# Weight-block sums three units ahead of their splits in a Strassen-type feed-forward, and another order of its first units

## The chip, the core and the metric

The kernel runs on one core of a Trainium2 chip. Its time is device microseconds (us) of one launch; the median of several runs is given, and of one of its executions the hardware profiler took the trace that is read here. Engines are named as in the profile: PE is TensorE's matmul, PEld its weight load, DVE is VectorE, ACT is ScalarE, POOL is GpSimd, SP is SyncE, whose queue asks for the weight transfers.

## What is computed

Two layers of a decoder trunk on 256 tokens of width 1024, all in fp32. Each layer is a feed-forward (FFN), a mixer, a cross-attention and a second FFN:

```python
def swiglu(x, w_gate, w_up, w_down):
    return (jax.nn.silu(x @ w_gate) * (x @ w_up)) @ w_down

for l in range(DEPTH):
    h = h + 0.5 * swiglu(rms_norm(h, ffn1_norm[l]), ffn1_w_gate[l], ffn1_w_up[l], ffn1_w_down[l])
    h = h + hybrid_mixer(rms_norm(h, mix_norm[l]), w_in[l], ssm_lambda_re[l], ssm_lambda_im[l],
...
    h = h + memory_cross_attention(rms_norm(h, xattn_norm[l]), rms_norm(mem, mem_norm[l]),
...
    h = h + 0.5 * swiglu(rms_norm(h, ffn2_norm[l]), ffn2_w_gate[l], ffn2_w_up[l], ffn2_w_down[l])
return rms_norm(h, final_norm)
```

DEPTH is 2, D_MODEL 1024 and D_FF is 2816. Only the second FFN of each layer is touched.

## The kernel before

**Units.** Every weight matrix comes as a stream of blocks of 128 x 1024 fp32 (512 KB). One block makes one unit of work: SP asks for its transfer into a `raw` buffer (4 of them), ScalarE rounds it to a high part `whi`, VectorE subtracts that from the block and so makes a low part `wlo` (5 buffers of each), and TensorE multiplies with high and low parts of the activations, three matmuls (high x high, high x low, low x high) for each product wanted. A plain unit is 12 matmuls of 128 x 512. `split_whole` writes the two instructions that split a block, `load_to` asks for transfers up to a few units ahead.

**The order** of the work is written out by the program on the host: a planner (`Clock`) keeps a model of the time of each engine, and by it places splits, evacuations and matmuls one behind the other. Each engine then runs its own list in that order. `feed` writes the split of a unit when it is due, up to 4 us of the model ahead and as far as the 5 buffers go.

**The second FFN** has 11 chunks of 256 columns of gate and of up. Its order of units is the string `SECOND`: P4 is a unit of the gate-and-up projection of chunk 4 (four make a chunk), D0 one of the down projection of chunk 0 (two make a chunk, into PSUM tiles `acc`), S2 is one product of the pair of chunks 2 and 3. P's matmuls go to the PSUM tiles `mm` (2 buffers), which ScalarE and VectorE empty into `z` (silu times up); TensorE transposes z (`tp<-ident,z`), and ScalarE and VectorE split the result into `gT`, the operand of D.

**The pairs.** Chunks 2 and 3, and chunks 7 and 8, are each computed as one Strassen-type product: seven products of half matrices instead of eight. Each takes two units of 6 matmuls, and its result goes to a PSUM tile `tp`. The table `PAIR` holds them in order: Q3, Q1, Q7, Q6, Q2, Q5, Q4. The weight operands are four blocks, X, P, Y, Q, two units each, and sums of them that VectorE makes in place:

- Q3 uses X, Q1 uses P, Q2 uses Q as they are loaded.
- Q7 uses X after X = X + Y; Q6 uses X after X = X + P; Q5 uses Y after Y = Y + P; Q4 uses X after X = X + Q.

In the names of the profile these are `blkX`, `blkP`, `blkY`, `blkQ`; X and Y lie in fixed places, P and Q in a pool of twelve slots (`s4`). In `split_whole` the sum of a unit stands right ahead of its own split: sum on VectorE, high part on ScalarE, low part on VectorE. In `load_to` each of Q3, Q1, Q7 and Q2 brings one block (both its units); Q6, Q5 and Q4 bring none.

The activations' own combinations (`xf`, `ef`, then high and low parts `eh`, `el`) are made in `combos`, started when chunk 0 is projected; Q3 needs the first of them. The results of the seven products are copied or added into `qs` on ScalarE and VectorE, and `chunk_done` transposes them (`tp<-ident,qs`) into `gT`.

Lines: L268 is VectorE's recorder, L305 ScalarE's, L344 the matmul, L355 the transpose, L557 the weight transfers.

Of the kernel before, what the change touches and what calls it, by code (L numbers as in the profile page):

```python
# [11 lines left out]
F32 = mybir.dt.float32  # L12
# [4 lines left out]
ALU = mybir.AluOpType  # L17
# [31 lines left out]


SECOND = (
# [3 lines left out]
)  # L55

PAIR = (
    ("Q3", (1, 1), "X", "X", None),
    ("Q1", (0, 0), "P", "P", None),
    ("Q7", (1, 0), "Y", "X", "Y"),  # L60
    ("Q6", None, None, "X", "P"),
    ("Q2", (0, 1), "Q", "Q", None),
    ("Q5", None, None, "Y", "P"),
    ("Q4", None, None, "X", "Q"),
)


def second_items():

    seen = {}  # L70
    for item in SECOND.split():
        k = seen[item] = seen.get(item, -1) + 1
        yield item[0], int(item[1:]), k
# [29 lines left out]
def stream_plan():  # L103

    plan = []
    for l in range(L):
        def ffn(nm):
            for j in range(NCH):
                for kp in range(4):
                    plan.append((nm + "_gu", l, 4 * j + kp, "A", (nm, l, 2 * kp), 4 if j == 0 and len(plan) >= 4 else 1))  # L110
                if j >= LAG:
                    for f in range(2):
                        plan.append((nm + "_dn", l, 2 * (j - LAG) + f, "B", None, 1))
            for n in range(2 * (NCH - LAG), 2 * NCH):
                plan.append((nm + "_dn", l, n, "B", None, 2 * LAG))

        def second(nm):
            for kind, j, k in second_items():
                if kind == "P":
                    plan.append((nm + "_gu", l, 4 * j + k, "A", None, 4 if j == 0 else 1))  # L120
                elif kind == "D":
                    plan.append((nm + "_dn", l, 2 * j + k, "B", None, 1))
                else:
                    _, block, to, operand, add = PAIR[k]
                    for u in range(2):
                        n = None if block is None else 4 * (j + block[0]) + 2 * block[1] + u
                        plan.append((nm + "_gu", l, n, "S", ((l, j), u, to, operand, add), 1))
            for n in range(2 * (NCH - LAG), 2 * NCH):
                plan.append((nm + "_dn", l, n, "B", None, 2 * LAG))

        def chunk(nm, c, norm, skew):
            for kp in range(4):
                plan.append((nm, l, 4 * c + kp, "A", (norm, l, 2 * kp), skew))

        ffn("ffn1")
        for c in range(4):
            chunk("w_in", c, "mix", 4 if c == 0 else 1)
        for c in range(3):
            chunk("wkv", c, "mem", 1)
        for k in range(4):  # L140
            plan.append(("w_glu", l, k, "B", None, 4))
        for k in (4, 5, 6, 7, 0, 1, 2, 3):
            plan.append(("w_out", l, k, "B", ("ssm", l, k) if k < 4 else ("sub", l, 0), 4))
        for c in range(2):
            chunk("wq", c, "xattn", 4 if c == 0 else 1)
        chunk("wkv", 3, "mem", 1)
        for k in range(8):
            plan.append(("wo", l, k, "B", None, 4))
        second("ffn2")
    need, at, i = [], 0.0, 0  # L150
    while i < len(plan):
        n = plan[i][5]
        need += [at + STEP * k for k in range(n)]
        at += STEP if plan[i][3] == "S" else 2 * STEP * n
        i += n
    return plan, need


class Task:


    def __init__(self, gen, now):
        self.gen, self.t, self.done, self.waiters = gen, now, False, []
        self.pe = -1.0
# [195 lines left out]
class Trunk:  # L360
    def __init__(self, ctx, tc, io):
        self.tc, self.io = tc, io
        self.c = Clock(tc.nc)
        self.v, self.a, self.g, self.p = Vector(self.c), Scalar(self.c), Pool(self.c), Tensor(self.c)
        P = lambda name, bufs, **kw: ctx.enter_context(tc.tile_pool(name=name, bufs=bufs, **kw))
        self.const = P("const", 1)
        self.xp = P("xp", 2)
        self.rawp = P("raw", N_RAW)
        self.hip = P("hi", N_W)
        self.lop = P("lo", N_W)  # L370
        self.tab = P("tab", 1)
        self.s4 = P("s4", N_S4)
        self.zp = P("zp", 4)
        self.gp = P("gp", 2)
        self.tp5 = P("tp5", N_T5)
        self.jp = P("jp", 1)
        self.sm = P("sm", 4)
        self.sp1 = P("sp1", 1)
        self.acc = P("acc", 4, space=bass.MemoryType.PSUM)
        self.mm = P("mm", 2, space=bass.MemoryType.PSUM)  # L380
        self.tp = P("tp", 1, space=bass.MemoryType.PSUM)
        self.dram = P("dram", 1, space=bass.MemoryType.DRAM)
        self.plan, self.need = stream_plan()
        self.main = 0.0
        self.upos = self.nload = self.nsplit = self.nfree = 0
        self.raw, self.w, self.blk = {}, {}, {}
        self.stream = Task(None, 0.0)
        self.nacc = self.nmm = 0
        self.accfree = [0.0, 0.0]
        self.mmfree = [0.0, 0.0]  # L390
        self.tpfree, self.tpown = [0.0, 0.0], {}
# [131 lines left out]
    def split_whole(self, i):  # L523
        hi = self.hip.tile([128, 1024], F32R, tag="hi", name="whi")
        lo = self.lop.tile([128, 1024], F32R, tag="lo", name="wlo")
        self.stream.t = 0.0
        kind, op = self.plan[i][3:5]
        if kind == "S":
            pair, u, _, operand, add = op
            r = self.blk[pair, operand, u]  # L530
            if add is not None:
                self.v.tensor_tensor(r, r, self.blk[pair, add, u], op=ALU.add)
        else:
            r = self.raw.pop(i)
        self.split(hi, lo, r)
        self.w[i] = [hi, lo, self.stream.t, self.stream.t]

    def load_to(self, m):
        while self.nload < min(m, len(self.plan)):
            i = self.nload  # L540
            self.nload += 1
            _, _, n, kind, op, _ = self.plan[i]
            if n is None:
                continue
            if kind != "S":
                r = self.rawp.tile([128, 1024], F32, tag="raw", name="raw")
                self.raw[i] = r
            else:
                pair, u, to = op[:3]
                if to in "PQ":  # L550
                    r = self.s4t([128, 1024], name="blk" + to)
                else:
                    if u == 0:
                        self.blk[pair, to] = self.tab.tile([128, 2, 1024], F32, tag={"X": "tB", "Y": "tD"}[to], name="blk" + to)
                    r = self.blk[pair, to][:, u, :]
                self.blk[pair, to, u] = r
            self.tc.nc.sync.dma_start(r, self.io["wst"][self.nwst])  # L557
            self.nwst += 1

    def split_unit(self, i, q):  # L560
        kind, gain = self.plan[i][3:5]
# [1298 lines left out]
def lay_out(a):  # L1860
# [7 lines left out]
    def type_b(w):  # L1868
        return w.reshape(-1, 128, 1024)

    groups = {}
    for l in range(L):
        for nm in ("ffn1", "ffn2"):
            g = f[nm + "_w_gate"][l].reshape(D, NCH, 1, 256)
            u = f[nm + "_w_up"][l].reshape(D, NCH, 1, 256)
# [5 lines left out]
        groups["wo", l] = type_b(f["xattn_wo"][l])  # L1881
        groups["w_glu", l] = type_b(f["ssm_w_glu"][l])
        groups["w_out", l] = type_b(f["w_out"][l])
    wst = np.concatenate([groups[s, l][n:n + 1] for s, l, n, _, _, _ in stream_plan()[0] if n is not None], axis=0)
    col = lambda v: v.reshape(-1, 128).T
    gains = np.concatenate(
        [col(f[k][l]) for l in range(L)
# [30 lines left out]
```

## Time and profile before

| | |
|---|---|
| Median of 3 runs | 1239.87 us (1234.87 to 1244.61) |
| Profiled execution | 1238.06 us, span 1236.3 us |
| Second FFN of layer 0, first to last product | 444 to 588 us of the span |
| Second FFN of layer 1, first to last product | 1051 to 1197 us |
| Granted TensorE clock, mean of the span | 0.994 |

A row of a group gives the busy time and the mean of one instruction; a row of the waits gives who waited for whom, us in total, times, longest. A row of the timeline is start, duration, engine, line, operation, output<-inputs and, in brackets, how long its engine was idle before it and what ended that. TensorE's matmuls overlap: its pace is read from start to start.

### The profile page before, as it was taken

What the parts mean: (1) busy time and instruction counts of PE and PEld (TensorE: products, weight loads), DVE (VectorE), ACT (ScalarE), POOL (GpSimd) and SP (SyncE); (2) the same over time, 40 slices, a digit from 0 to 9 for tenths busy, and PEclk for the clock granted to TensorE, in tenths of its full rate; (3) what the DMA queues carried; (4) which work ended last, traced back from release to release, by engine and by line L of the source; (5) the groups of instructions that cost most, each with busy time, mean ns of one, the idle gap of its engine ahead of it and who ended that gap; (6) DMA issues with size and microseconds to landing.
All of it is one profiled execution on the core that took longest, in us unless ns stands there. A gap on an engine that the chain in (4) does not pass through costs nothing.

```text
span 1236.3 us, 17726 instructions
## 1 busy us (share of the span) xinstructions
PE 1201.5 (97%) x6580; PEld 973.4 (79%) x6580; DVE 904.8 (73%) x1498; ACT 711.1 (58%) x1206; POOL 45.1 (4%) x104
## 2 busy tenths in 40 slices
PE   9999999999999999998999999999999999999987
PEld 7888888777888877776888887887678888777766
DVE  5797776597867587867678877656977667786775
ACT  6665455567766555554555644655686656545543
POOL 2100001000000000000010000100000000000000
PEclk9999999999999999999999999999999999998999
DMA  8655557543644564453565655664445446545532
GB/s 282 214 187 182 163 151 208 150 140 117 194 159 145 184 224 153 172 186 119 184 200 183 193 160 160 186 192 141 125 160 175 155 149 225 174 151 213 166 114 86
DMA packets 59974, 210.91 MB, mean 171 GB/s; under 512 B 7168, under 2 KB 8288, under 8 KB 59888
## 3 DMA queue, kind: packets, MB, share of 16 engines
q1 hardware_dynamic: 56304, 202.92, 50.9%
q0 software_dynamic: 2000, 5.24, 1.4%
q10 hardware_dynamic: 1584, 1.62, 0.5%
q8 instruction: 51, 0.84, 0.3%
q14 instruction: 35, 0.29, 0.1%
HBM read 207.00 MB, written 1.05 MB: 168 GB/s over the span
## 4 chain that ended last, share of the span: by engine, by line
PE 81%; DVE 11%; ACT 4%; issue 2%; DMA 1%; ACTq 0%; POOLq 0%; POOL 0%; DVEq 0%
PE mm L344 42%; PE acc L344 29%; PE tp L344 6%; PE tp L355 5%; DVE wlo L268 5%; ACT whi L305 3%; DVE blkX L268 2%; DMA uq<-z 1%; DVE blkY L268 1%; DVE qs L268 1%; DVE p L268 1%; DVE gT L268 1%; DMA h<-in_x 0%; DVE z L268 0%; DVE xf L268 0%
## 5 line engine op out<-in xcount | busy, mean ns | idle before, releaser
L268 DVE SCALAR_TENSOR_TENSOR wlo<-raw,gains,whi 128x512 fp32r<-128x512 f32 x368 | 263.1, 747 | 92.9 <-ACT whi L305 91.5
L344 PE MATMUL mm<-whi,xh 128*128 128x512 f32 x768 | 308.0, 401 | 0.0
L344 PE MATMUL mm<-wlo,xh 128*128 128x512 f32 x768 | 300.6, 392 | 0.3 <-DVE wlo L268 0.3
L344 PE MATMUL mm<-whi,xl 128*128 128x512 f32 x768 | 300.8, 392 | 0.0
L305 ACT ACTIVATE whi<-raw,gains 128x512 fp32r<-128x512 f32 x368 | 240.9, 713 | 14.3 <-DMA raw<-in_wst 5.7
L344 PE MATMUL acc<-whi,gT 128*128 128x512 f32 (+1 forms) x712 | 237.7, 396 | 0.0
L268 DVE TENSOR_TENSOR wlo<-raw,whi 128x512 fp32r<-128x512 f32 (+1 forms) x236 | 209.0, 912 | 29.0 <-ACT whi L305 27.9
L305 ACT ACTIVATE whi<-raw 128x512 fp32r<-128x512 f32 (+1 forms) x236 | 181.0, 805 | 45.6 <-DMA raw<-in_wst 18.9
L344 PEld LDWEIGHTS mm<-whi,xh 128*128 128x128 f32 x768 | 145.3, 189 | 31.5 <-issue 1.3
L344 PEld LDWEIGHTS mm<-whi,xl 128*128 128x128 f32 x768 | 144.9, 189 | 30.8
L344 PEld LDWEIGHTS mm<-wlo,xh 128*128 128x128 f32 x768 | 145.3, 189 | 28.6 <-DVE wlo L268 0.8
L344 PEld LDWEIGHTS acc<-whi,gT 128*128 128x128 f32 x712 | 133.2, 188 | 26.6
L344 PE MATMUL acc<-wlo,gT 128*128 128x512 f32 (+1 forms) x356 | 138.0, 388 | 0.0
L344 PE MATMUL mm<-whi,mem 128*128 128x512 f32 x256 | 92.6, 409 | 0.0
L344 PEld LDWEIGHTS acc<-wlo,gT 128*128 128x128 f32 x356 | 67.1, 188 | 12.0
L305 ACT ACTIVATE sg<-mm,rstd 128x256 f32<-128x256 f32 x44 | 20.9, 474 | 87.1 <-PE mm L344 87.0
L305 ACT ACTIVATE whi<-blkX 128x1024 fp32r<-128x1024 f32 x32 | 33.6, 1057 | 55.0 <-DVE blkX L268 55.0
L268 DVE TENSOR_TENSOR wlo<-blkX,whi 128x1024 fp32r<-128x1024 f32 x32 | 39.2, 1225 | 33.7 <-ACT whi L305 33.7
L344 PEld LDWEIGHTS mm<-whi,mem 128*128 128x128 f32 x256 | 48.1, 188 | 11.5 <-issue 1.3
L344 PE MATMUL mm<-wlo,mem 128*128 128x512 f32 x128 | 50.9, 398 | 3.9 <-DVE wlo L268 3.9
L305 ACT ACTIVATE xh<-tp 128x512 fp32r<-128x512 f32 x32 | 19.1, 596 | 58.7 <-PE tp L355 58.7
L305 ACT ACTIVATE z<-mm,rstd 128x256 f32<-128x256 f32 (+1 forms) x52 | 29.4, 568 | 39.5 <-PE mm L344 38.9
(256 smaller groups left out, 1531.2 us busy)
## 6 DMA issues: line engine op xcount, KB each, us to landing
raw<-in_wst SPq DMA_DIRECT2D x350, 512.0 KB, 4.2
blkX<-in_wst SPq DMA_DIRECT2D x8, 512.0 KB, 5.2
blkP<-in_wst SPq DMA_DIRECT2D x8, 512.0 KB, 6.4
blkY<-in_wst SPq DMA_DIRECT2D x8, 512.0 KB, 5.6
blkQ<-in_wst SPq DMA_DIRECT2D x8, 512.0 KB, 5.4
raw<-in_wst SPq DMA_DIRECT2D x4, 256.0 KB, 5.4
mem<-in_mem POOLq DMA_DIRECT2D x2, 512.0 KB, 7.4
uq<-z ACTq DMA_DIRECT2D x8, 128.0 KB, 4.6
```

Of the source, the lines that this page charges most:

```text
L268: r = getattr(self.e, name)(*a, **k)
L305: r = self.e.activation(out, in_, func, **k)
L344: r = self.e.matmul(out, lhsT, rhs, **k)
L355: r = self.e.transpose(out, in_, ident)
```

## The change

It does three things.

1. `split_whole` writes the sum of a unit (now in `add_block`) not only ahead of its own split: behind the split of every unit i it also writes the sums of those among the next three units (`EARLY = 3`) whose operands are already loaded and whose in-place block is no longer wanted in its earlier state. A sum that was written early is not written again.
2. In `PAIR`, Q1 now brings P and Y together, unit by unit, and Q7 brings Q; Q2 brings none.
3. `SECOND` puts P4 D0 P4 D0 ahead of the first product of the first pair, and moves a few other P and D units among the products up to S7's second; behind that it is as before.

```diff
 SECOND = (
-    "P0 P0 P0 P0 P1 P1 P1 P1 "
...
+    "P0 P0 P0 P0 P1 P1 P1 P1 P4 D0 P4 D0 "
...
 PAIR = (
-    ("Q3", (1, 1), "X", "X", None),
-    ("Q1", (0, 0), "P", "P", None),
-    ("Q7", (1, 0), "Y", "X", "Y"),
...
+    ("Q3", (("X", 1, 1),), "X", None),
+    ("Q1", (("P", 0, 0), ("Y", 1, 0)), "P", None),
+    ("Q7", (("Q", 0, 1),), "X", "Y"),
...
+EARLY = 3
...
         if kind == "S":
             pair, u, _, operand, add = op
+            self.add_block(i)
             r = self.blk[pair, operand, u]
-            if add is not None:
-                self.v.tensor_tensor(r, r, self.blk[pair, add, u], op=ALU.add)
+            self.content[pair, operand, u] = i
         else:
             r = self.raw.pop(i)
         self.split(hi, lo, r)
+        for j in range(i + 1, min(i + 1 + EARLY, len(self.plan))):
+            if self.plan[j][3] == "S":
+                self.add_block(j)
...
+    def add_block(self, i):
+
+        pair, u, _, operand, add = self.plan[i][4]
+        if add is None or i in self.added or (pair, add, u) not in self.blk:
+            return
+        last = [j for j in range(i) if self.plan[j][3] == "S" and self.plan[j][4][0] == pair and self.plan[j][4][1] == u
+                and operand in (self.plan[j][4][3], self.plan[j][4][4])]
+        if any(j not in self.added and self.plan[j][4][4] is not None for j in last):
+            return
+        if any(self.plan[j][4][3] == operand and self.content.get((pair, operand, u), -1) < j for j in last):
+            return
+        self.added.add(i)
+        r = self.blk[pair, operand, u]
+        self.v.tensor_tensor(r, r, self.blk[pair, add, u], op=ALU.add)
```

What it does to the lists of the engines is seen at three places of the first pair in layer 0; the other pair and the other layer are alike. The line numbers of the changed kernel are one higher in the recorders (L269 for L268, L345 for L344), and 22 higher at the transfers.

VectorE around Q4, the last product of the first pair, before:

```order
L268 TENSOR_TENSOR gT<-tp,gT 128x512
L268 TENSOR_TENSOR blkX<-blkX,blkQ 128x1024
L268 TENSOR_TENSOR wlo<-blkX,whi 128x1024
L268 TENSOR_TENSOR blkX<-blkX,blkQ 128x1024
L268 TENSOR_TENSOR wlo<-blkX,whi 128x1024
L268 SCALAR_TENSOR_TENSOR qs<-qs,rstd 128x256 x2
```

And in the changed kernel, from the second low part of Q5 on:

```order
L269 TENSOR_TENSOR wlo<-blkY,whi 128x1024
L269 TENSOR_TENSOR blkX<-blkX,blkQ 128x1024
L269 SCALAR_TENSOR_TENSOR qs<-qs,rstd 128x256
L269 TENSOR_TENSOR wlo<-raw,whi 128x1024
L269 TENSOR_TENSOR blkX<-blkX,blkQ 128x1024
L269 TENSOR_TENSOR wlo<-raw,whi 128x1024
L269 SCALAR_TENSOR_TENSOR qs<-tp,qs 128x512
L269 TENSOR_TENSOR qs<-qs,tp 128x512
L269 TENSOR_TENSOR wlo<-blkX,whi 128x1024 x2
```

The two sums stand between the splits of the units ahead (`wlo<-raw` are D4 and P6), and the two low parts of Q4 follow each other.

TensorE at the end of P1, before (`tp<-whi,eh` is the first matmul of Q3):

```order
L344 MATMUL mm<-whi,xl 128x512
L355 MATMUL tp<-ident,z 128x128 x4
L344 MATMUL tp<-whi,eh 128x512
L344 MATMUL tp<-wlo,eh 128x512
L344 MATMUL tp<-whi,el 128x512
```

And in the changed kernel, from the first matmuls of P4 on:

```order
L345 MATMUL mm<-whi,xh 128x512
L345 MATMUL mm<-wlo,xh 128x512
L345 MATMUL mm<-whi,xl 128x512
L356 MATMUL tp<-ident,z 128x128 x2
L345 MATMUL mm<-whi,xh 128x512
L345 MATMUL mm<-wlo,xh 128x512
L345 MATMUL mm<-whi,xl 128x512
L356 MATMUL tp<-ident,z 128x128 x2
```

The transposes of z are split in two between matmuls of P4; the first `tp<-whi,eh` comes 12 matmuls of P4, 12 of D0, 12 of P4 and 12 of D0 behind the end of P1.

SP's queue at the first pair, before:

```order
L557 DMA raw<-in_wst 128x1024 x132
L557 DMA blkX<-in_wst 128x1024 x2
L557 DMA raw<-in_wst 128x1024 x3
L557 DMA blkP<-in_wst 128x1024 x2
L557 DMA raw<-in_wst 128x1024 x2
L557 DMA blkY<-in_wst 128x1024 x2
L557 DMA raw<-in_wst 128x1024 x5
L557 DMA blkQ<-in_wst 128x1024 x2
```

And in the changed kernel:

```order
L579 DMA raw<-in_wst 128x1024 x136
L579 DMA blkX<-in_wst 128x1024 x2
L579 DMA raw<-in_wst 128x1024 x2
L579 DMA blkP<-in_wst 128x1024
L579 DMA blkY<-in_wst 128x1024
L579 DMA blkP<-in_wst 128x1024
L579 DMA blkY<-in_wst 128x1024
L579 DMA raw<-in_wst 128x1024 x2
L579 DMA blkQ<-in_wst 128x1024 x2
```

The blocks of the pair come closer together, with 4 plain blocks between the first X and the first Q where there were 10.

More of the change, by code (lines that the diff above doesn't have):

```diff
@@ L51 @@
 SECOND = (
[3 rows of a table removed]
[3 rows of a table added]
 )
 PAIR = (
-    ("Q3", (1, 1), "X", "X", None),
-    ("Q1", (0, 0), "P", "P", None),
-    ("Q7", (1, 0), "Y", "X", "Y"),
[L61 to L64, printed above, removed]
+    ("Q3", (("X", 1, 1),), "X", None),
+    ("Q1", (("P", 0, 0), ("Y", 1, 0)), "P", None),
+    ("Q7", (("Q", 0, 1),), "X", "Y"),
+    ("Q6", (), "X", "P"),
+    ("Q2", (), "Q", None),
+    ("Q5", (), "Y", "P"),
+    ("Q4", (), "X", "Q"),
 )
+EARLY = 3
 def second_items():
@@ L123, in second @@
                 else:
-                    _, block, to, operand, add = PAIR[k]
+                    _, loads, operand, add = PAIR[k]
                     for u in range(2):
-                        n = None if block is None else 4 * (j + block[0]) + 2 * block[1] + u
-                        plan.append((nm + "_gu", l, n, "S", ((l, j), u, to, operand, add), 1))
+                        n = [4 * (j + a) + 2 * b + u for _, a, b in loads]
+                        plan.append((nm + "_gu", l, n, "S", ((l, j), u, [x[0] for x in loads], operand, add), 1))
             for n in range(2 * (NCH - LAG), 2 * NCH):
@@ L386, in __init__ @@
         self.raw, self.w, self.blk = {}, {}, {}
+        self.added, self.content = set(), {}
         self.stream = Task(None, 0.0)
@@ L541, in load_to @@
             self.nload += 1
-            _, _, n, kind, op, _ = self.plan[i]
-            if n is None:
+            kind, op = self.plan[i][3:5]
+            if kind != "S":
+                r = self.raw[i] = self.rawp.tile([128, 1024], F32, tag="raw", name="raw")
+                self.fetch(r)
                 continue
[L545 to L549, printed above, removed]
+            pair, u, loads = op[:3]
+            for to in loads:
                 if to in "PQ":
@@ L556, in load_to, with fetch @@
                 self.blk[pair, to, u] = r
-            self.tc.nc.sync.dma_start(r, self.io["wst"][self.nwst])
-            self.nwst += 1
+                self.fetch(r)
+    def fetch(self, r):
+        self.tc.nc.sync.dma_start(r, self.io["wst"][self.nwst])
+        self.nwst += 1
     def split_unit(self, i, q):
@@ L1883, in lay_out @@
         groups["w_out", l] = type_b(f["w_out"][l])
-    wst = np.concatenate([groups[s, l][n:n + 1] for s, l, n, _, _, _ in stream_plan()[0] if n is not None], axis=0)
+    wst = np.concatenate([groups[s, l][i:i + 1] for s, l, n, _, _, _ in stream_plan()[0] for i in (n if isinstance(n, list) else [n])], axis=0)
     col = lambda v: v.reshape(-1, 128).T
```

4 rows, old and new, of the table SECOND are left out of this document.

## The prediction

> **What bounds the kernel now.** I read the page first, then the waits of TensorE, then TensorE's own timeline at the longest waits, then VectorE and ScalarE at the same place, and last two windows over the second feed-forward (FFN) of each layer. The page and the list of TensorE's waits (engine, what waited, on whom: us in total, times, longest):
>
> ```profile
> span 1236.3 us, 17726 instructions
> PE 1201.5 (97%) x6580; PEld 973.4 (79%) x6580; DVE 904.8 (73%) x1498; ACT 711.1 (58%) x1206; POOL 45.1 (4%) x104
> ...
> PE tp L344 <- DVE wlo L268: 10.7, 16, 0.8
> PE tp L344 <- ACT whi L305: 4.7, 8, 0.9
> PE mm L344 <- DVE wlo L268: 4.1, 5, 1.4
> PE tp L344 <- ACT eh L305: 2.4, 2, 1.2
> PE tp L355 <- ACT up L305: 1.6, 2, 1.0
> PE tp L355 <- DVE z L268: 1.4, 2, 0.7
> ```
>
> TensorE is the bound, and the matmuls into `tp` at L344, the seven products of a pair of chunks, are its largest named waiters. Four of these rows belong to the places that the change edits: 16 + 8 + 2 + 2 = 28 waits, 14 in each layer, 10.7 + 4.7 + 2.4 + 1.4 = 19.2 us idle. What one looks like, on TensorE (start, duration, what, idle before it):
>
> ```profile
> 508.31 0.43 PE L344 MATMUL tp<-whi,xh 128*128 128x512 f32 x1
> 509.50 0.51 PE L344 MATMUL tp<-wlo,xh 128*128 128x512 f32 x1 [0.76 <-DVE wlo L268]
> ...
> 510.53 0.39 PE L344 MATMUL tp<-whi,xl 128*128 128x512 f32 x1
> 511.79 0.50 PE L344 MATMUL tp<-whi,xh 128*128 128x512 f32 x1 [0.87 <-ACT whi L305]
> 513.05 0.50 PE L344 MATMUL tp<-wlo,xh 128*128 128x512 f32 x1 [0.76 <-DVE wlo L268]
> ...
> 454.21 2.72 PE acc L344 x12
> ```
>
> The last row, from the chain of work, gives the pace: 2.72 / 12 = 0.227 us from start to start. So 508.31 to 509.50 lost 1.19 - 0.23 = 0.96 us where the list says 0.76: about 0.2 us of each wait hides under the modelled end of the matmul before. Why it waits, from VectorE and ScalarE:
>
> ```profile
> 505.82 1.22 DVE L268 TENSOR_TENSOR blkX<-blkX,blkQ 128x1024 f32<-128x1024 f32 x1
> 507.13 1.06 ACT L305 ACTIVATE whi<-blkX 128x1024 fp32r<-128x1024 f32 x1 [2.83 <-DVE blkX L268]
> 508.22 1.23 DVE L268 TENSOR_TENSOR wlo<-blkX,whi 128x1024 fp32r<-128x1024 f32 x1 [1.19 <-ACT whi L305]
> 509.37 1.22 DVE L268 TENSOR_TENSOR blkX<-blkX,blkQ 128x1024 f32<-128x1024 f32 x1
> ```
>
> Sum, high part, low part run one behind the other: from sum to sum 509.37 - 505.82 = 3.55 us a unit, while TensorE uses up a unit of a product (6 matmuls) in 1.36. VectorE sits idle 1.19 of the 3.55. The two windows, from the first product to the last, overall (columns PE, PEld, DVE, ACT, POOL busy with counts, clock, DMA) and for the transposes alone:
>
> ```profile
> 444.00:588.00 144.00, 134.24 (x585) 106.21 (x585) 109.21 (x118) 74.80 (x93) 0.00 (x0) 1.00 0.46 162
> 1051.00:1197.00 146.00, 136.46 (x584) 107.91 (x583) 108.83 (x118) 74.03 (x92) 0.00 (x0) 0.98 0.47 162
> ...
> 444.00:588.00 144.00, 4.75 (x28) 3.52 (x28) 1.00 0.46 162
> ```
>
> In layer 0, 585 - 28 = 557 matmuls at 0.227 need 126.4 us. A transpose has a quarter of a matmul's columns (0.06 us) and a mean of 4.75 / 28 = 0.17 busy; I take 0.11, so 3.1. Of 144 us, 144 - 129.5 = 14.5 are lost; in layer 1, with 584 - 28 = 556, 146 - 129.3 = 16.7. VectorE is busy 109.2 of 144: it has the time, in the wrong order.
>
> Layer 1 loses more because the clock falls right behind the same cluster of waits (last two rows: windows, with TensorE's count and clock):
>
> ```profile
> 1120.23 0.79 PE L344 MATMUL tp<-wlo,xh 128*128 128x512 f32 x1 [0.53 <-DVE wlo L268]
> 1120.82 0.63 PE L344 MATMUL tp<-whi,xl 128*128 128x512 f32 x1
> 1121.25 0.63 PE L344 MATMUL tp<-whi,xh 128*128 128x512 f32 x1
> ...
> 1125.93 0.39 PE L344 MATMUL mm<-whi,xh 128*128 128x512 f32 x1
> ...
> 1197.00:1203.00 6.00, 6.00 (x23) 4.80 (x23) 5.70 (x9) 4.10 (x6) 0.00 (x0) 0.72 0.53 166
> 1119.00:1127.00 8.00, 7.47 (x21) 5.63 (x22) 6.99 (x9) 5.58 (x8) 0.00 (x0) 0.57 0.72 263
> ```
>
> From 1120.23 to 1125.93 stand 11 matmuls and 4 transposes, 11 x 0.227 + 0.44 = 2.94 us at full pace: 2.76 lost. In 1197 to 1203, 19 matmuls and 4 transposes need 4.75 of 6.0: 1.25 lost. Together 4.0 us.
>
> **The change, part by part.** *Amount of work.* Matmuls, splits, the 32 sums (four kinds, eight of each) and the transfers stay the same in number and size; only places move. So nothing is added to TensorE, and what can be won is waiting.
>
> *Sums three units ahead.* A sum now stands on VectorE behind the split of a unit up to three earlier, with one or two other splits between it and its own high part. Its durations:
>
> ```profile
> L305 ACT ACTIVATE whi<-blkX x32: 1047/1059/1062, 438.0 to 1194.3; 128x1024 fp32r<-128x1024 f32 x32
> L268 DVE TENSOR_TENSOR wlo<-blkX,whi x32: 1217/1226/1227, 440.9 to 1195.4; 128x1024 fp32r<-128x1024 f32 x32
> L268 DVE TENSOR_TENSOR blkX<-blkX,blkQ x8: 1210/1218/1221, 505.8 to 1193.0; 128x1024 f32<-128x1024 f32 x8
> ...
>   ACT whi L305: 33.7, 26
> ```
>
> (The last row is VectorE's idle time in this tile's operations while it waited for ScalarE's high part, in us and times.)
>
> A unit of a product then costs VectorE 2 x 1.2 = 2.4 us instead of 3.55, ScalarE's 1.06 lies beside it. Against TensorE's 1.36 that is still short by 1.0 a unit, 2.1 a product, but each plain unit between products gives TensorE 2.72 us for VectorE's 1.2, that is 1.5 back, and five high/low buffers let the splits run ahead. I carried the new order of layer 0 on by hand from 443.8, each instruction starting when its engine, its operand and its buffer are free, at 1.2 us for a full VectorE operation, 1.0 to 1.06 for ScalarE, 2.72 for a TensorE unit, 0.45 for four transposes. Low part of a product's second unit ready, against TensorE getting there: Q3 455.0 / 458.0, Q1 463.4 / 466.1, Q7 472.3 / 474.8, Q6 480.2 / 483.0, Q2 488.1 / 491.1, Q5 498.1 / 499.8, Q4 507.1 / 508.0; in the second pair Q6 542.4 / 545.0, Q5 561.5 / 564.6, Q4 571.1 / 572.6. All are in time; the thinnest is the plain unit behind Q5 of the first pair (501.0 / 501.3). So 24 of the 28 waits go.
>
> *Four units put before the first pair.* The other four waits are the start of Q3:
>
> ```profile
> 444.97 0.39 PE L344 MATMUL mm<-whi,xl 128*128 128x512 f32 x1
> 446.06 0.83 PE L355 MATMUL tp<-ident,z 128*128 128x128 f32 x4 [0.70 <-DVE z L268]
> 448.09 0.50 PE L344 MATMUL tp<-whi,eh 128*128 128x512 f32 x1 [1.20 <-ACT eh L305]
> ```
>
> Now P4, D0, P4, D0 (10.9 us) stand there, and the transposes of z go between their halves. P4 needs a PSUM buffer that the first z frees: by hand at 445.0, before TensorE asks at 445.2; the second at 446.5 against 446.8. The four `eh` are done at 452 against 456.6. These waits go too. The cover is those four units; the next thing late would be Q3's low part, with 3 us in hand.
>
> *Two blocks with the second product.* P and Y are asked for alternately on SP's queue, Y one product earlier than before. SP, and landings:
>
> ```profile
> 513.02 0.80 SPq L557 DMA_DIRECT2D blkX<-in_wst  x2
> ...
> DMA to landing us min/median/max: 4.0/5.6/6.7
> ```
>
> The second pair is the crowded place: X can only be asked for when Q4 of the first pair has read it (before: 513.0; by hand now 507.2), then two plain units, P, Y, P, Y, two plain units and Q: ten blocks of 512 KB ahead of the ones that follow. At 263 GB/s (the 1119 window) one takes 2.0 us; Y is then there at about 507 + 8 x 2.0 + 2 = 525, against its sum at 526. I count no wait, with 1 us in hand.
>
> *Sum.* 19.2 + 28 x 0.2 = 24.8 us of waits, and 4.0 of clock, since what precedes both falls is the run of waits: 28.8. The windows give 14.5 + 16.7 + 1.25 = 32.4 as the most. What stays or is new: transposes of the last quarter `qs` (0.4 by hand), the thin unit behind Q5 (0 to 0.5), small waits by SP; I take 1.4 a layer, 2.8, between 0 and 7. The profiled execution took 1238.06 us, its span and 1.8 around it; the median of the runs shown, 1239.87, lies 0.15% higher. 1238.1 - 28.8 + 2.8 = 1212.
>
> **The Trainium skill on two of these.** On the clock, the row above has it fall behind waits of under 1.3 us each. The Trainium skill, "TensorE: Matmul & The Clock Gate", section on the HAM clock gate, names an idle window of about 3.4 us for a fall; taken so, these waits would not be its cause and the 4.0 us would stay: 1216. The trace speaks against that reading, since both falls come at once behind the longest clusters, Q4 of either pair, though the same clusters in layer 0 have none. The same page, in its section on the array as 16 sub-arrays, says that ScalarE's and VectorE's queues are strictly first in, first out; that rule speaks against this change, for a sum placed early whose block is late holds every split behind it. It would give the last rival below, 1250.
>
> **Rivals.**
> - *Half stays.* VectorE is busy 109.2 us of what would be 129.5, 84%, and every sum put ahead delays the split behind it by 1.2. My margins near Q5 and Q4 (0.3 to 1.5 us) are of that size. If one pair of each layer keeps its waits: 28.8 / 2, 1238.1 - 14.4 = 1224. Against it: the hand account uses 1.2 where VectorE starts full operations every 1.15 (508.22 to 509.37).
> - *The waits only change their name*: the evacuations of `tp` and the z's, in order between the splits, set the pace, and the early sums sit behind them: 1238, no change. For it: VectorE's splits do stand behind such operations; against it: its idle time in the chain (1.19 a unit) is waiting for ScalarE on the sum, not for TensorE.
> - *Slower.* One mechanism: Y's landing. Its sum comes before the splits of plain units, so every us it is late is a us for all. Four places (two pairs, two layers). To lose 1% over the present time each would have to cost (28.8 + 12) / 4 = 10 us, Y landing 11 us later than counted, nearly twice the longest landing shown (6.7); then 1250.
>
> **Chances.** Near all goes 68%, own range 1205 to 1219; half stays 18%, 1219 to 1229; no change 10%, about 1238; slower 4%, 1250. About 1% is what a measurement here can tell from no change, so faster means under 1227.5: the first case and 16 of the 18: 84%; same 12%; slower 4%. The range from 1205 to 1227 leaves out the last two cases and the edges of the first two. The low end is the ceiling of the windows, 1238.1 - 32.4.
>
> **What would show it.** In the new profile the four rows of waits should hold under 3 us together; in the windows over the products VectorE's idle time for ScalarE in this tile's view (33.7) should be a third or less; the clock should stay at 1.00 in layer 1; the first `tp<-whi,eh` should follow a D0 unit without a wait. A wait of `blkX<-blkX,blkY` on a transfer, or TensorE waiting in the plain units between products, would show me wrong.

## The result and the profile after

| | before | changed |
|---|---|---|
| Median of 4 runs | 1238.34 us (1234.87 to 1244.61) | 1204.38 us (1202.78 to 1206.80) |
| Ratio, with its 95% interval | | 0.9722 (0.9678 to 0.9766) |
| Profiled execution | 1238.06 us, span 1236.3 | 1206.80 us, span 1203.7 |

The kernel is 34.0 us faster by the medians, 31.3 by the two profiled executions and 32.6 by their spans. The forecast was 26: the sign and the mechanism came out, the size was too small, and 1204.38 lies just under the low end of the range, 1205.

The page of the changed kernel, its span, its busy times and its chain of work:

```profile
span 1203.7 us, 17730 instructions
...
PE 1187.4 (99%) x6580; PEld 971.2 (81%) x6580; DVE 903.1 (75%) x1498; ACT 711.2 (59%) x1206; POOL 45.1 (4%) x104
...
PE 94%; DVE 2%; DMA 2%; ACT 1%; issue 1%; ACTq 0%; POOLq 0%; POOL 0%; DVEq 0%
```

The other engines do what they did before (VectorE 903.1 us against 904.8). The chain that ended last now lies on TensorE for 94% of the span and on VectorE for 2%. All of TensorE's waits in the changed kernel (who waited for whom, us, times, longest):

```profile
PE mm L345 <- DVE wlo L269: 4.2, 5, 1.4
PE tp L356 <- DMA h<-in_x: 1.5, 1, 1.5
PE tp L356 <- ACT up L306: 1.5, 2, 0.8
PE pz L345 <- DVE zero L269: 1.2, 1, 1.2
```

The four rows with the 28 waits are gone, and no new row has come. These four were there before, and lie in other stages. VectorE's idle time for ScalarE in the operations of `blkX`, 33.7 us in 26 times before, is down to a quarter, as the prediction asked:

```profile
  ACT whi L306: 8.7, 10
```

The start of Q3 came as forecast too: its first matmul follows the last one of D0 without a wait.

```profile
457.01 0.39 PE L345 MATMUL acc<-whi,gT 128*128 128x512 f32 x1
457.24 0.39 PE L345 MATMUL tp<-whi,eh 128*128 128x512 f32 x1
```

The windows over the products, now shorter, in layer 0 and layer 1 (columns as before):

```profile
444.00:575.00 131.00, 131.00 (x594) 108.05 (x593) 111.51 (x121) 77.48 (x96) 0.00 (x0) 1.00 0.55 195
1037.00:1168.00 131.00, 131.00 (x594) 108.06 (x593) 111.44 (x122) 77.76 (x96) 0.00 (x0) 1.00 0.55 195
```

And the first of them for the transposes alone:

```profile
444.00:575.00 131.00, 5.59 (x32) 4.30 (x32) 1.00 0.55 195
```

TensorE is busy without a break and the clock stays at 1.00 in both. By the pace used before, 594 - 32 = 562 matmuls at 0.227 and 32 transposes at 0.11 need 127.6 + 3.5 = 131.1 of 131.0 us: no waiting is left to win here. VectorE at Q4 of the first pair, from its timeline (start, duration, what):

```profile
498.02 1.22 DVE L269 TENSOR_TENSOR blkX<-blkX,blkQ 128x1024 f32<-128x1024 f32 x1
499.15 0.47 DVE L269 SCALAR_TENSOR_TENSOR qs<-qs,rstd 128x256 f32<-128x256 f32 x1
499.55 1.21 DVE L269 TENSOR_TENSOR wlo<-raw,whi 128x1024 fp32r<-128x1024 f32 x1
500.68 1.22 DVE L269 TENSOR_TENSOR blkX<-blkX,blkQ 128x1024 f32<-128x1024 f32 x1
501.82 1.21 DVE L269 TENSOR_TENSOR wlo<-raw,whi 128x1024 fp32r<-128x1024 f32 x1
...
504.15 2.35 DVE L269 TENSOR_TENSOR wlo<-blkX,whi 128x1024 fp32r<-128x1024 f32 x2
```

And TensorE's timeline where Q4 starts:

```profile
507.21 0.39 PE L345 MATMUL tp<-whi,xh 128*128 128x512 f32 x1
507.44 0.39 PE L345 MATMUL tp<-wlo,xh 128*128 128x512 f32 x1
```

No bracket of idle time stands behind either. Both low parts are ready at 506.5; TensorE asks for the first at 507.44.

### The profile page after: what moved, and what is told of

It reads as the page before. It is cut to its first block, busy times and chain, and to the rows that moved or that the text cites. A ratio compares the mean times of both kernels' runs of the same rounds, so it can differ in the third digit from the quotient of the medians.

```text
span 1203.7 us, 17730 instructions
## 1 busy us (share of the span) xinstructions
PE 1187.4 (99%) x6580; PEld 971.2 (81%) x6580; DVE 903.1 (75%) x1498; ACT 711.2 (59%) x1206; POOL 45.1 (4%) x104
## 3 DMA queue, kind: packets, MB, share of 16 engines
HBM read 207.00 MB, written 1.05 MB: 173 GB/s over the span
## 4 chain that ended last, share of the span: by engine, by line
PE 94%; DVE 2%; DMA 2%; ACT 1%; issue 1%; ACTq 0%; POOLq 0%; POOL 0%; DVEq 0%
PE mm L345 48%; PE acc L345 33%; PE tp L345 8%; PE tp L356 5%; DMA uq<-z 1%; DVE wlo L269 1%; DVE p L269 1%; DMA h<-in_x 0%; ACT whi L306 0%; DVE nm L269 0%; ACT junk L306 0%; ACT z L306 0%; ACT up L306 0%; ACTq L315 0%; DVE h L269 0%
## 5 line engine op out<-in xcount | busy, mean ns | idle before, releaser
L269 DVE SCALAR_TENSOR_TENSOR wlo<-raw,gains,whi 128x512 fp32r<-128x512 f32 x368 | 263.0, 747 | 92.2 <-ACT whi L306 90.7
L345 PE MATMUL mm<-whi,xh 128*128 128x512 f32 x768 | 307.0, 400 | 0.0
L345 PE MATMUL mm<-whi,xl 128*128 128x512 f32 x768 | 300.0, 391 | 0.0
L345 PE MATMUL mm<-wlo,xh 128*128 128x512 f32 x768 | 299.3, 390 | 0.3 <-DVE wlo L269 0.3
L345 PE MATMUL acc<-whi,gT 128*128 128x512 f32 (+1 forms) x712 | 238.9, 396 | 0.0
L269 DVE TENSOR_TENSOR wlo<-raw,whi 128x512 fp32r<-128x512 f32 (+1 forms) x236 | 209.7, 911 | 20.9 <-ACT whi L306 19.7
L345 PEld LDWEIGHTS mm<-whi,xh 128*128 128x128 f32 x768 | 144.5, 188 | 31.4 <-issue 1.3
L345 PEld LDWEIGHTS mm<-whi,xl 128*128 128x128 f32 x768 | 144.3, 188 | 30.6
L345 PEld LDWEIGHTS mm<-wlo,xh 128*128 128x128 f32 x768 | 144.8, 189 | 28.0 <-DVE wlo L269 0.6
L345 PEld LDWEIGHTS acc<-whi,gT 128*128 128x128 f32 x712 | 133.2, 188 | 26.3
L345 PE MATMUL acc<-wlo,gT 128*128 128x512 f32 (+1 forms) x356 | 138.0, 388 | 0.0
L345 PE MATMUL mm<-whi,mem 128*128 128x512 f32 x256 | 92.6, 410 | 0.0
L345 PEld LDWEIGHTS acc<-wlo,gT 128*128 128x128 f32 x356 | 67.1, 189 | 11.7
L306 ACT ACTIVATE gT<-tp 128x512 fp32r<-128x512 f32 x44 | 26.3, 598 | 56.4 <-PE tp L356 56.4
L345 PEld LDWEIGHTS mm<-whi,mem 128*128 128x128 f32 x256 | 48.1, 188 | 11.4 <-issue 1.3
L345 PE MATMUL mm<-wlo,mem 128*128 128x512 f32 x128 | 51.0, 398 | 3.9 <-DVE wlo L269 3.9
L269 DVE TENSOR_TENSOR gT<-tp,gT 128x512 fp32r<-128x512 f32 x44 | 30.2, 687 | 21.7 <-ACT gT L306 21.7
```

What stands on the lines that cost most here:

```text
L269: r = getattr(self.e, name)(*a, **k)
L306: r = self.e.activation(out, in_, func, **k)
L345: r = self.e.matmul(out, lhsT, rhs, **k)
```

## The experiments

Nine kernels, each timed in three rounds beside the kernel before, in three sittings on one chip each; the kernel before had 1237.07 us beside the first four, 1236.85 beside the next four and 1237.21 beside the last.

| kernel | median us | ratio to before (95%) |
|---|---|---|
| early sums; order and loads of before | 1212.62 | 0.9799 (0.9785 to 0.9814) |
| new order and loads; no sum ahead | 1233.33 | 0.9968 (0.9954 to 0.9983) |
| early sums and new loads; order of before | 1211.89 | 0.9795 (0.9778 to 0.9811) |
| changed kernel with the loads of before | 1203.88 | 0.9729 (0.9715 to 0.9744) |
| sums at most one unit ahead | 1212.81 | 0.9803 (0.9788 to 0.9818) |
| sums at most two units ahead | 1203.79 | 0.9731 (0.9716 to 0.9745) |
| every sum done twice | 1224.77 | 0.9898 (0.9884 to 0.9913) |
| sums on GpSimd | 1230.32 | 0.9942 (0.9925 to 0.9958) |
| no lead, both sums of a product together | 1204.28 | 0.9732 (0.9706 to 0.9759) |

### The three parts apart

**Early sums alone**: `SECOND` and the loads of before, `EARLY = 3` kept.

```diff
-    ("Q1", (("P", 0, 0), ("Y", 1, 0)), "P", None),
-    ("Q7", (("Q", 0, 1),), "X", "Y"),
...
-    ("Q2", (), "Q", None),
...
+    ("Q1", (("P", 0, 0),), "P", None),
+    ("Q7", (("Y", 1, 0),), "X", "Y"),
...
+    ("Q2", (("Q", 0, 1),), "Q", None),
```

> Sums up to three units ahead, with the order of units and the loads of before. Theory A (the sum's place makes 24 of the 28 waits and with them the falls of the clock; the order of units makes only the 4 at the start of Q3): the rows of TensorE's waits on wlo and whi for tp go, those on eh and z (2.4 and 1.4 us) stay; about 1211 us. Rival B (it is the new order of units, with more plain units between the products, that gives VectorE room, and early sums alone sit behind evacuations): under half of the gain, 1222 us or more, with waits on wlo for tp still there.

Measured 1212.62: theory A, within 2 us. Its waits on TensorE for `tp` are, beside those of other stages, the ones foretold and no others (theory A had no fall of the clock at this place; there were two, read below, so part of the agreement with 1211 is luck):

```profile
PE tp L345 <- ACT eh L306: 2.4, 2, 1.2
...
PE tp L356 <- DVE z L269: 1.4, 2, 0.7
```

**Order and loads alone**: the sums back in their old place.

```diff
-EARLY = 3
+EARLY = 0
```

> The new order of units and the new loads, each sum right ahead of its own split as before. Theory A: only the 4 waits at the start of Q3 go, about 5 us, the other 24 stay: 1233 us (1226 to 1236). Rival B: most of the gain is here, 1222 us or less.

Measured 1233.33, theory A again. The rows of `eh` and `z` are gone, those on the split are all there:

```profile
PE tp L345 <- DVE wlo L269: 10.5, 16, 0.8
PE tp L345 <- ACT whi L306: 5.7, 8, 0.9
```

**Early sums and new loads, order of before**: only `SECOND` put back.

```diff
-    "P0 P0 P0 P0 P1 P1 P1 P1 P4 D0 P4 D0 "
+    "P0 P0 P0 P0 P1 P1 P1 P1 "
...
```

> Early sums and the new loads, with the order of units of before. Theory A: the loads give nothing, so as with the early sums alone, within 2 us of it (about 1211 us). Rival C (the sum of Q7 waits for Y's landing unless Y comes with P): 3 us or more under the run with early sums alone, which would then show waits of blkX<-blkX,blkY on a transfer.

**The loads of before alone**: the changed kernel with the `PAIR` of the first diff above.

> The changed kernel with the loads of before: one block with each of Q3, Q1, Q7 and Q2. Theory A: as the changed kernel, 1204 us within 2. Rival C: 1207 us or more, VectorE's sums of X and Y wait for Y's transfer.

Measured 1211.89 and 1203.88: 0.7 us and 0.5 us from the runs that they are compared with. The loads give nothing. The order of units is worth 1212.62 - 1203.88 = 8.7 us once the sums are early, and 3.7 (1237.07 - 1233.33) without. What the 8.7 consist of shows in the run with early sums alone, on TensorE at the start of Q3:

```profile
444.37 0.39 PE L345 MATMUL mm<-whi,xl 128*128 128x512 f32 x1
445.45 0.83 PE L356 MATMUL tp<-ident,z 128*128 128x128 f32 x4 [0.70 <-DVE z L269]
447.48 0.80 PE L345 MATMUL tp<-whi,eh 128*128 128x512 f32 x1 [1.20 <-ACT eh L306]
448.08 0.63 PE L345 MATMUL tp<-wlo,eh 128*128 128x512 f32 x1
448.50 0.63 PE L345 MATMUL tp<-whi,el 128*128 128x512 f32 x1
...
450.21 0.63 PE L345 MATMUL tp<-whi,eh 128*128 128x512 f32 x1
450.64 0.45 PE L345 MATMUL tp<-wlo,eh 128*128 128x512 f32 x1
450.92 0.39 PE L345 MATMUL tp<-whi,el 128*128 128x512 f32 x1
```

And two windows of the same run, around the start of Q3 in either layer:

```profile
446.00:451.00 5.00, 3.80 (x11) 2.73 (x11) 4.44 (x7) 3.62 (x6) 0.00 (x0) 0.66 0.75 296
1043.00:1049.00 6.00, 4.86 (x13) 3.54 (x14) 4.25 (x7) 3.59 (x7) 0.00 (x0) 0.72 0.62 240
```

From 448.08 on the matmuls go at 0.43 us instead of 0.227, and the clock of the two windows (0.66, 0.72) says why: it fell behind these two waits, in both layers. From 444.37 to 450.92 stand 9 matmuls and 4 transposes, 9 x 0.227 + 0.44 = 2.48 us at full pace; they took 6.55, so 4.1 us were lost in this layer. 2.4 of them had gone by 447.48, in the waits (3.11 less 0.67 of work); nearly all of the other 1.6 is the clock. Layer 1 lost 4.4 us, counted the same way from 1040.98 to 1048.06. Together that is 8.5 of the measured 8.7. In the kernel before, the same two waits left the clock at 1.00 in both layers; why it fell here is not shown.

### How far ahead a sum has to stand

**At most one unit, and at most two** (the second with `EARLY = 2`).

```diff
-EARLY = 3
+EARLY = 1
```

> The changed kernel with sums at most one unit ahead. Theory A (what counts is that another split stands between a sum and its own high part): with one unit no split comes between, the chain sum, high part, low part stays, so as with none ahead, about 1232 us. Rival E (the gain grows with the lead): a third of the 29 us between none and three, about 1224 us.

> The changed kernel with sums at most two units ahead: one split stands between each sum and its own high part. Theory A: full gain, 1204 us within 2, no wait on wlo or whi for tp. Rival E: two thirds, about 1214 us.

Two units gave 1203.79, as theory A had it. One unit gave 1212.81, and neither theory had that: 1232 was wrong by 19 us, 1224 by 11. VectorE's idle time for ScalarE in the operations of `blkX` fell only by a fifth. Without a lead, in the tile's view (us, times):

```profile
  ACT whi L306: 31.5, 26
```

With one unit:

```profile
  ACT whi L306: 25.1, 20
```

But TensorE's waits in the run with one unit fell from 24 to these 10:

```profile
PE tp L345 <- DVE wlo L269: 5.8, 8, 0.8
...
PE tp L345 <- ACT whi L306: 0.3, 2, 0.2
```

So the chain of sum, high part and low part stays with one unit of lead, as theory A said, and yet costs less than a third of what it did: 8.4 us over the changed kernel, where no lead costs 29.0. The first sum of a product starts earlier there, at three of the four sums of the first pair ahead of evacuations that stood before it. The second unit still comes 3.56 us behind the first (504.55 to 508.11 at Q4 of the first pair, in that run's trace), but the waits left are eight on a low part, four in each layer. VectorE's idle time is not TensorE's.

**Both sums of a product together, no lead.** This takes the other half alone: the chain is broken, and nothing is moved ahead of the product's first split.

```diff
-EARLY = 3
+EARLY = 0
...
             self.add_block(i)
+            if u == 0:
+                self.add_block(i + 1)
```

> The changed kernel with no lead, but both sums of a product written together, right ahead of its first split: sum, sum, low part, low part. The first low part then stands where it stood with none ahead, the second 2.4 us earlier. Theory H (it is the second unit that comes late, 3.55 us behind the first where TensorE takes 1.36; the lead itself matters little): almost all waits on whi and wlo for tp go, 1206 us within 2.5. Rival I (sums must also be moved ahead in time, as the run with one unit ahead suggests): half or more of the waits stay, 1215 us or more.

Measured 1204.28, the full gain, theory H. One wait of 0.3 us on `wlo` for `tp` is left in its trace:

```profile
PE tp L345 <- DVE wlo L269: 0.3, 1, 0.3
```

The two low parts of Q4 of the first pair, on VectorE in that run:

```profile
504.32 2.36 DVE L269 TENSOR_TENSOR wlo<-blkX,whi 128x1024 fp32r<-128x1024 f32 x2
```

What hurt was the second unit, 3.55 us behind the first, where TensorE wants it 1.36 us behind; writing sum, sum, low, low brings it to about 1.15 behind. The lead of three units is one way to do that, not the reason. All this is shown with the new order of units; with the order of before, the two sums together were not run.

### How much room VectorE has

**Every sum done twice**, the order of all else the same.

```diff
         self.v.tensor_tensor(r, r, self.blk[pair, add, u], op=ALU.add)
+        self.v.e.tensor_tensor(r, r, r, op=ALU.max)
```

> The changed kernel with a second VectorE operation of the same size behind each of the 32 sums (the block's maximum with itself, which changes nothing), order of all else the same: 8 x 1.2 = 9.8 us more on VectorE a pair, 2.4 us a product. If the margins are as thin as the hand account in the prediction had them (0.3 to 3 us), waits on wlo for tp come back at 8 or more products, 1215 us or more. Rival F (VectorE has more room than that, since each operation was counted 0.05 too long): under 1210 us.

Measured 1224.77: 39 us more work on VectorE cost 20.4 us against the changed kernel. The time was over 1215 as written for thin margins, but not by the waits named there: `tp` never waits for a low part, TensorE waits elsewhere. Its longest rows of waits (of the 5.8 us on `mm`, 4.2 were there in the changed kernel):

```profile
PE tp L356 <- DVE z L269: 9.5, 8, 1.7
PE mm L345 <- DVE wlo L269: 5.8, 9, 1.4
PE acc L345 <- DVE wlo L269: 2.0, 4, 0.5
```

A window over most of the products of layer 0 in that run:

```profile
444.00:580.00 136.00, 129.28 (x572) 103.28 (x571) 124.50 (x131) 74.88 (x93) 0.00 (x0) 1.00 0.52 181
```

VectorE is busy 124.5 of 136 us there and late with whatever stands behind an early sum: the z's and the plain units. The time is that of the rival "half stays" in the prediction (1224), but not its mechanism, since none of the 28 waits is kept: at a load of 92% instead of 85%, about half of the added work hides and half does not.

**Sums on GpSimd**, up to five units ahead, which takes 39 us of sums off VectorE. Two things change at once here, the engine and the lead.

```diff
-EARLY = 3
+EARLY = 5
...
-        self.v.tensor_tensor(r, r, self.blk[pair, add, u], op=ALU.add)
+        self.g.tensor_tensor(r, r, self.blk[pair, add, u], op=ALU.add)
```

> The changed kernel with the sums on GpSimd and up to five units ahead, which takes 39 us of work off VectorE. Theory A (in the second feed-forward nothing is left to win but 0.9 us): 1204 us within 2 if GpSimd's sum is done in time, slower by the waits on it if not. Rival G (VectorE is still what delays TensorE): 1202 us or less.

Measured 1230.32, 26 us slower than on VectorE. Neither theory had that: no wait in the trace is put down to a sum of GpSimd's, so the sums were in time, and yet TensorE waits for low parts (`tp` for `wlo`: 7.7 us in 8 times). VectorE's timeline ahead of Q6 of the first pair:

```profile
469.21 2.36 DVE L269 TENSOR_TENSOR wlo<-blkX,whi 128x1024 fp32r<-128x1024 f32 x2 [1.50 <-ACT whi L306]
471.49 6.76 DVE L269 TENSOR_TENSOR wlo<-raw,whi 128x1024 fp32r<-128x1024 f32 x2
```

And GpSimd's:

```profile
470.52 6.65 POOL L329 TENSOR_TENSOR blkX<-blkX,blkP 128x1024 f32<-128x1024 f32 x2 [10.78 <-DVE wlo L269]
```

Two low parts take 2.36 us in the row before GpSimd's sums are under way (its record opens 1.05 us before that row ends) and 6.76 beside them. Moving the sums off VectorE does not free it. Whether it would have been faster with VectorE free is not answered by this run, since it never was.

## Why the prediction was right in kind and too small in size

The places and the reason of the waits were right. Two terms of the sum failed, both in size: what stays or is new (2.8 us forecast, 0 measured) and what the 28 waits cost (24.8 forecast, 28.1 measured). They make 6.1 of the 7.7 us between 1212.1 and 1204.38; 0.5 is not accounted for, and 1.1 is the place of the median within the spread of runs, for which the low end of the range left nothing.

- *Sums three units ahead take 24 of 28 waits; four units ahead of Q3 take the other 4.* Right: the first two experiments split them just so. What the prediction took as the reason, 2.4 us of VectorE a unit instead of 3.55, is what the run with both sums together confirms; the lead itself was not needed. The account by hand was good to about 0.6 us: it had Q4's second low part ready at 507.1 and TensorE there at 508.0; the trace has 506.5 and 508.12. Its start of Q3, 456.6, is 457.24 in the trace, with this profile's second FFN beginning some 0.6 us later.
- *What stays or is new, 2.8 us.* This is the term that failed first. My account by hand had found 0.4 us of wait at one place a layer, and allowances on top made it 1.4. The changed kernel's list has no such wait: 0 instead of 2.8.
- *About 0.2 us of each wait hide.* This term, with the 19.2 us listed 24.8, was too small as well. Read from start to start on TensorE before, the 28 waits cost 25.6 us. The matmul behind a wait is late too:

```profile
513.05 0.50 PE L344 MATMUL tp<-wlo,xh 128*128 128x512 f32 x1 [0.76 <-DVE wlo L268]
513.38 0.39 PE L344 MATMUL tp<-whi,xl 128*128 128x512 f32 x1
```

  From one start to the next are 0.33 us where 0.227 is the pace, another 0.1. 18 of the 28 waits have such a matmul behind them (the others have the next wait), which makes 2.0 us, and at the start of Q3 one more matmul is late by 0.2 in either layer. That is 28.1 us for the 24.8. The windows had shown it: their 32.4 exceeded the 28.8 by 3.6, and I called that a ceiling instead of asking what it was made of.
- *4.0 us of clock.* Right for this profile: the windows over the products stand at 1.00 now, and so does the stretch behind the second one, 1168 to 1174. It is one draw, though: in the executions of the kernel before that were timed beside the experiments, the mean clock of the span went from 0.998 (1234.87 us) to 0.990 (1240.68). Together 28.1 + 4.0 - 0 = 32.1 against 32.6 between the two spans.
- *The range.* Its low end was the ceiling of one execution, 1205.7, with nothing for the spread of runs, and the change took that ceiling whole: 1238.1 - 32.6 = 1205.5. The median lies 1.1 us under that. The profiled execution of the changed kernel is the slowest of its four (1206.80, median 1204.38), which is 2.4 of the 2.7 us between 31.3 and 34.0; the rest is the median of the kernel before. 1.3 us of its slowness lie outside the span: it took 3.1 us more than its span, where the other three executions, and the profiled one before, took 1.8 more. Its span, 1203.7, is the longest of four too (1201.0 to 1203.7); there TensorE waited 1.5 us for the input's transfer, against 0.7 in the trace before.
- *The loads cost nothing, with 1 us in hand.* Right as to the cost: with and without them the time is the same. The margin was larger: the second pair's Y in layer 0 was asked for from 509.31 on, its last block at 510.32, and with the longest landing below it was there by 521, not 525; the sum started at 526.29. Y's transfers did get slower to land, with a median of 8.9 us against 5.6 and no wait for it; from the tile's view of `blkY` in the changed kernel:

```profile
DMA to landing us min/median/max: 7.4/8.9/10.3
```

- *Rivals.* "Half stays" did not come: at VectorE's load of 85% (111.5 of 131) no wait is left in the products, while at 92%, with every sum done twice, TensorE waits again, for other operations. "The waits change their name" and "slower" have no row in the profile.
- *The Trainium skill on the clock.* The clock fell behind waits of 0.70 and 1.20 us, in both layers of the run with early sums alone, and behind waits of at most 0.84 us at Q4 of the first pair in layer 1 before. Both speak against reading the rule of the Trainium skill, "TensorE: Matmul & The Clock Gate" (section on the HAM clock gate), as needing one idle stretch of 3.4 us. The same clusters had no fall elsewhere (all of those in layer 0 before, and the start of Q3 in layer 1 before), so what else must come together stays open.

## What to carry to other kernels

Where one engine makes an operand by a chain over two others, look at the second of two operands that are wanted close together: writing the first steps of both before the second steps of either can be worth as much as a long lead, and here it was worth all of it. A listed wait can cost more than its idle time, here 25.6 us for 19.2: measure from start to start, and take in the instruction after it. When a count of lost time from pace and a list of waits differ, find out what the difference is made of before leaving it out of the sum; here it was real time. And where the forecast nears what can be won at most, the low end of the range needs room for the spread of runs under it.

## What the runs showed of the hardware that was not expected

- The granted clock fell to a half behind clusters of waits of 0.5 to 1.2 us each. Read in windows of 0.2 us it is 0.50 from 447.3 to 450.7 and from 1044.7 to 1048.1 in the run with early sums alone, and from 1119.1 to 1125.9 and 1197.5 to 1200.9 before. So 2.4 us of waiting at the start of Q3 cost 4.1.
- A GpSimd sum of 128x1024 fp32 and a VectorE subtraction of the same size that run at the same time take up to 3.4 us each; VectorE's takes 1.22 alone, and no run here has GpSimd's alone. The Trainium skill, "SBUF — State Buffer", in its part on the shared port pair, says that a VectorE operation with two inputs in SBUF and a GpSimd operation that reads SBUF lock each other out for a whole instruction; this trace agrees in so far as two subtractions take 6.76 us instead of 2.36 and the two sums beside them 6.65. That the two engines take whole instructions in turn is not seen in it.

```profile
L269 DVE TENSOR_TENSOR wlo<-blkX,whi x32: 1215/1224/3433, 451.2 to 1187.0; 128x1024 fp32r<-128x1024 f32 x32
...
L329 POOL TENSOR_TENSOR blkX<-blkX,blkP x8: 3302/3342/3393, 470.5 to 1149.1; 128x1024 f32<-128x1024 f32 x8
```

The two rows are the tile's view of the run with sums on GpSimd (shortest, median and longest in ns): the same VectorE operation runs from 1215 to 3433 ns.
